# Softmax with a temperature on one core: a one-row tail on the sixth chunk's load and a one-row head on the first chunk's store

## The chip, the cores and the metric

The kernel runs on one core of a Trainium2 chip. The metric is the device time of one execution in microseconds (us); the lower the better. The median of three runs of the kernel before the change is 162.11 us (162.08 to 162.43).

## What is computed

The reference is a softmax over the last axis with temperature 0.5:

```python
x = randn(16, 1024, 512)  # float32
x_scaled = x / 0.5
x_max = max(x_scaled, axis=-1, keepdims=True)
exp_x = exp(x_scaled - x_max)
out = exp_x / sum(exp_x, axis=-1, keepdims=True)  # float32
```

There are 16,384 rows of 512 elements, 2 KB each. The input and the output are 33.55 MB each, and every byte is moved once.

## The kernel before

**Tiling.** The rows are cut into eight chunks (C = 8). A chunk has 128 partitions with G = 16 consecutive rows each, so that a whole chunk is 4 MB, 32 KB a partition, contiguous in memory for each partition. Six buffers (BUFS) hold chunks; the seventh and the eighth chunk take the buffers of the first and the second. Everything is done in place: a chunk is loaded, turned into its softmax, and stored from the same buffer.

**Lists.** Three lists say how a chunk is cut, by rows of a partition. LOADS gives the DMAs of its load, BLOCKS the pieces in which it is computed, STORES the DMAs of its store. Before the change, the first chunk is loaded in two parts (the first 4 rows of a partition, then the other 12), the next six whole, the eighth without its last two rows (LATE), which come on the Pool queue. The first chunk is computed in three blocks and the last in two, which makes eleven blocks in all. Every chunk is stored whole.

**Queues.** `load` (L65 holds its DMA) issues the loads of the first six chunks from ScalarE's queue, all at the start and in order, and those of the last two chunks from SyncE's queue, where each waits until the buffer's old chunk has been stored. `store` (L144) issues every store from ScalarE's queue. In that queue's ring, then, seven load DMAs of six chunks stand first, and all eight stores follow. `load_last_rows` (L87, L93) issues the eighth chunk's last two rows from the Pool queue.

**Work on a block.** `shift` takes the negated row maximum on VectorE (L74) and doubles it (L78). `exponentials` runs one ScalarE instruction a row, exp(2x - 2max) with the row's sum on the side (L104). `scale_vector` takes the reciprocal of the sums (L121) and multiplies most rows by it on VectorE (L123); `scale_scalar` scales the last eighth of the rows on ScalarE (L134). A store follows when the chunk's last block is done.

**Order.** The order of each engine's instructions is written by hand (manual_schedule). A loop over the blocks i issues the exponentials of block i + 1, the scaling of block i on both engines, the maximum of block i + 2, and the store of block i. For the second chunk the last two rows' exponentials are put behind the store of the first chunk, on ScalarE's queue.

**Semaphores.** DMAs from ScalarE's and SyncE's queues count their completion on eight semaphores that are taken in turn; a DMA that takes a semaphore again has to come after the earlier DMA on it has completed. At the end SyncE waits for everything.

Of the kernel before, what the change touches and what calls it, by code (L numbers as in the profile page):

```python
# [1 line left out]

# [4 lines left out]


@with_exitstack
def kernel(  # L10
    ctx: ExitStack,
    tc: tile.TileContext,
    x: bass.AP,
    out: bass.AP,
):
    nc = tc.nc
    fp32 = mybir.dt.float32
    P = nc.NUM_PARTITIONS
    AX = mybir.AxisListType.X
    EXP = mybir.ActivationFunctionType.Exp  # L20
    COPY = mybir.ActivationFunctionType.Copy
    MAX = mybir.AluOpType.max

    D = x.shape[-1]
    xf = x.flatten_outer_dims()
    of = out.flatten_outer_dims()
    N = xf.shape[0]

    G = 16
    C = N // (P * G)
    assert C * P * G == N
    xr = xf.rearrange("(c p g) d -> c p g d", p=P, g=G)
    outr = of.rearrange("(c p g) d -> c p g d", p=P, g=G)
    WHOLE = [(0, G)]
    LATE = 2
    LOADS = [[(0, 4), (4, G)]] + [WHOLE] * 6 + [[(0, G - LATE)]]
    BLOCKS = [[(0, 4), (4, 8), (8, G)]] + [WHOLE] * 6 + [[(0, 8), (8, G)]]  # L40
    STORES = [WHOLE] * 8
    BMAX = 16
    BUFS = 6

    data = ctx.enter_context(tc.tile_pool(name="data", bufs=BUFS))
    stats = ctx.enter_context(tc.tile_pool(name="stats", bufs=6))

    ctx.enter_context(tc.manual_schedule())


    chunks = {}
    blocks = [(c, lo, hi) for c in range(C) for lo, hi in BLOCKS[c]]
    n = len(blocks)
    biases, sums, recips = {}, {}, {}

    finished = []
    def load(c):
        if c < BUFS:
            chunks[c] = data.tile([P, G, D], fp32, name="xt")
        else:  # L60
            chunks[c] = chunks[c - BUFS]
        xt = chunks[c]
        queue = nc.scalar if c < BUFS else nc.sync
        for lo, hi in LOADS[c]:
            part = queue.dma_start(out=xt[:, lo:hi, :], in_=xr[c][:, lo:hi, :])  # L65
            finished.append(part.ins.name)

    def shift(i):
        c, lo, hi = blocks[i]
        if c not in chunks:  # L70
            load(c)
        b = hi - lo
        negmax = stats.tile([P, BMAX], fp32, name="negmax")
        nc.vector.tensor_reduce(  # L74
            negmax[:, 0:b], chunks[c][:, lo:hi, :], axis=AX, op=MAX, negate=True
        )
        biases[i] = stats.tile([P, BMAX], fp32, name="bias")
        nc.vector.tensor_scalar_mul(biases[i][:, 0:b], negmax[:, 0:b], 2.0)  # L78

    def load_last_rows(signal):
        seen = stats.tile([P, 1], fp32, name="seen", bufs=1)
        copied = nc.gpsimd.tensor_copy(out=seen, in_=signal)  # L87
        finished.append(copied.ins.name)
        c = C - 1
        to = chunks[c - BUFS][:, G - LATE : G, :]  # L90
        of_ = xr[c][:, G - LATE : G, :]
        for p0, p1 in ((P - 2, P), (0, P - 2)):
            part = nc.gpsimd.dma_start(  # L93
                out=to[p0:p1], in_=of_[p0:p1], max_dma_last_dim=4 * D
            )
            finished.append(part.ins.name)

    def exponentials(i, rows):
        c, lo, hi = blocks[i]
        if i not in sums:  # L100
            sums[i] = stats.tile([P, BMAX], fp32, name="sums")
        for g in rows:
            row = chunks[c][:, lo + g, :]
            nc.scalar.activation(  # L104
                out=row,
                in_=row,
                func=EXP,
                bias=biases[i][:, g : g + 1],
                scale=2.0,
                accum_out=sums[i][:, g : g + 1],  # L110
            )
            if c == BUFS - 1 and g == 10:
                load_last_rows(sums[i][:, g : g + 1])


    def scale_vector(i):
        c, lo, hi = blocks[i]
        b = hi - lo
        k = b - b // 8
        recips[i] = stats.tile([P, BMAX], fp32, name="recip")  # L120
        nc.vector.reciprocal(recips[i][:, 0:b], sums[i][:, 0:b])  # L121
        rows = chunks[c][:, lo : lo + k, :]
        last = nc.vector.tensor_mul(  # L123
            rows, rows, recips[i][:, 0:k].unsqueeze(2).broadcast_to((P, k, D))
        )
        if i == n - 1:
            finished.append(last.ins.name)

    def scale_scalar(i):
        c, lo, hi = blocks[i]  # L130
        b = hi - lo
        for g in range(b - b // 8, b):
            row = chunks[c][:, lo + g, :]
            last = nc.scalar.activation(  # L134
                out=row, in_=row, func=COPY, scale=recips[i][:, g : g + 1]
            )
            if i == n - 1:
                finished.append(last.ins.name)

    def store(i):  # L140
        c, _, end = blocks[i]
        for lo, hi in STORES[c]:
            if hi == end:
                part = nc.scalar.dma_start(  # L144
                    out=outr[c][:, lo:hi, :], in_=chunks[c][:, lo:hi, :]
                )
                if c < C - 1:
                    finished.append(part.ins.name)

    load(0)  # L150
    warm = stats.tile([P, 1], fp32, name="warm", bufs=1)
    nc.vector.memset(warm, 0.0)  # L152
    nc.scalar.activation(out=warm, in_=warm, func=EXP)  # L153
    for c in range(1, BUFS):
        load(c)

    shift(0)
    shift(1)

    def rows(i):  # L160
        c, lo, hi = blocks[i]
        cut = hi - lo - (2 if c == 1 else 0)
        return range(cut), range(cut, hi - lo)

    exponentials(0, rows(0)[0])
    for i in range(n):
        if i + 1 < n:
            exponentials(i + 1, rows(i + 1)[0])
        scale_vector(i)
        scale_scalar(i)  # L170
        if i + 2 < n:
            shift(i + 2)
        store(i)
        if i + 1 < n:
            exponentials(i + 1, rows(i + 1)[1])

    seen = nc.sync.nop()
    info = mybir.DependencyInfo(
        mybir.DependencyClass.Sync, mybir.DependencyReason.DATA
    )  # L180
    for name in finished:
        tc.add_manual_dep(seen.ins, name, info, reason="leaves one wait for the end")


# [1 line left out]
_INS = ['x']  # L186
_OUTS = [((16, 1024, 512), 'float32')]


# [23 lines left out]
```

## Time and profile before

| what | value |
| --- | --- |
| median of the runs | 162.11 us |
| profiled execution, its own time | 162.08 us |
| span from its first instruction to its last | 160.2 us |
| bytes moved | 67.13 MB, half read from memory, half written |
| mean DMA rate over the span | 419 GB/s |
| ScalarE queue's ring (q10) | 2160 packets, 58.72 MB |
| SyncE queue's ring (q1) | 288 packets, 7.86 MB |
| Pool queue's ring (q0) | 192 packets, 0.52 MB |

The profile shows one execution. DVE is VectorE, ACT is ScalarE, POOL is GpSimd, SP is SyncE. Each row of the sliced view divides the span into 40 equal slices of 4.0 us; a digit is the busy share in tenths, and the GB/s row gives what the 16 DMA engines moved in a slice. A window's row gives its start and end in us and its length, then for VectorE, ScalarE and GpSimd the busy time and the number of instructions, then the clock, the DMA busy share and the GB/s. A DMA packet is counted in the window in which it starts, so a share can be over 1. A transfer is made of packets, one a partition here, and ends on each DMA engine with a packet of 4 bytes that counts its completion. The chain of waits lists start, duration and instruction of the chain of work that ended last.

### The profile page before, as it was taken

What the parts mean: (1) busy time and instruction counts of PE and PEld (TensorE: products, weight loads), DVE (VectorE), ACT (ScalarE), POOL (GpSimd) and SP (SyncE); (2) the same over time, 40 slices, a digit from 0 to 9 for tenths busy, and PEclk for the clock granted to TensorE, in tenths of its full rate; (3) what the DMA queues carried; (4) which work ended last, traced back from release to release, by engine and by line L of the source; (5) the groups of instructions that cost most, each with busy time, mean ns of one, the idle gap of its engine ahead of it and who ended that gap; (6) DMA issues with size and microseconds to landing.
All of it is one profiled execution on the core that took longest, in us unless ns stands there. A gap on an engine that the chain in (4) does not pass through costs nothing.

```text
span 160.2 us, 410 instructions
## 1 busy us (share of the span) xinstructions
DVE 134.6 (84%) x45; ACT 102.2 (64%) x273; POOL 1.9 (1%) x7
## 2 busy tenths in 40 slices
DVE  0607999999999999999999999999999999958000
ACT  3071549069989972998199909991899891690000
POOL 0000000000000000000000000040000000000000
DMA  5999999999999997999999999999999999999995
GB/s 184 470 401 507 401 393 499 417 393 468 442 401 442 466 401 303 475 393 434 475 401 417 475 409 417 444 459 394 428 456 436 397 466 450 393 442 466 401 401 245
DMA packets 2642, 67.13 MB, mean 419 GB/s; under 512 B 336, under 2 KB 336, under 8 KB 464
## 3 DMA queue, kind: packets, MB, share of 16 engines
q10 hardware_dynamic: 2160, 58.72, 86.0%
q1 hardware_dynamic: 288, 7.86, 11.4%
q0 software_dynamic: 192, 0.52, 0.8%
q14 instruction: 2, 0.02, 0.0%
HBM read 33.55 MB, written 33.55 MB: 419 GB/s over the span
## 4 chain that ended last, share of the span: by engine, by line
DVE 76%; DMA 7%; issue 5%; ACT 3%; ACTq 0%
DVE negmax L74 42%; DVE xt L123 32%; DMA xt<-in_x_dram 7%; ACT xt L104 3%; DVE bias L78 1%; DVE recip L121 1%; ACTq L65 0%
## 5 line engine op out<-in xcount | busy, mean ns | idle before, releaser
L104 ACT ACTIVATE xt<-xt,bias 128x512 f32<-128x512 f32 x128 | 90.4, 708 | 40.7 <-DVE bias L78 39.8
L74 DVE TENSOR_REDUCE negmax<-xt 128x16 f32<-128x8192 f32 (+2 forms) x11 | 69.9, 6353 | 9.5 <-DMA xt<-in_x_dram 9.5
L123 DVE TENSOR_TENSOR xt<-xt,recip 128x7168 f32<-128x7168 f32 (+2 forms) x11 | 62.0, 5637 | 0.4
L104 ACT ACTIVATION_READ_ACCUMULATOR xt<-xt,bias 128x1 f32 x128 | 23.9, 187 | 0.0
L134 ACT ACTIVATE xt<-xt,recip 128x512 f32<-128x512 f32 x15 | 9.9, 706 | 0.0
L121 DVE RECIPROCAL recip<-sums 128x16 f32<-128x16 f32 (+2 forms) x11 | 2.4, 219 | 1.8 <-ACT xt L104 1.8
L153 ACT ACT_TABLE_LOAD x1 | 1.3, 1283 | 1.6 <-PEq L197 1.6
L78 DVE TENSOR_SCALAR bias<-negmax 128x16 f32<-128x16 f32 (+2 forms) x11 | 1.9, 173 | 0.4
L93 POOL DMA_DIRECT2D xt<-in_x_dram x2 | 1.5, 741 | 0.5 <-issue 0.5
L87 POOL COPY seen<-sums 128x1 f32<-128x1 f32 x1 | 0.2, 184 | 103.7 <-ACT xt L104 103.7
L152 DVE MEMSET warm<- 128x1 f32 x1 | 0.1, 59 | 0.8 <-PEq L197 0.8
L153 ACT ACTIVATE warm<-warm 128x1 f32<-128x1 f32 x1 | 0.2, 202 | 0.0
L197 POOL MEMSET const-bfloat16-1.0<- 128x1 bf16 x1 | 0.1, 96 | 0.0
L197 POOL MEMSET const-uint8-127<- 128x1 uint8 x1 | 0.1, 96 | 0.0
L197 POOL MEMSET const-float32-0.0<- 128x1 f32 x1 | 0.1, 93 | 0.2 <-issue 0.2
L197 POOL MEMSET const-float32-1.0<- 128x1 f32 x1 | 0.1, 93 | 0.0
## 6 DMA issues: line engine op xcount, KB each, us to landing
out_dram<-xt ACTq DMA_DIRECT2D x8, 4096.0 KB, 24.9
xt<-in_x_dram ACTq DMA_DIRECT2D x5, 4096.0 KB, 39.5
xt<-in_x_dram SPq DMA_DIRECT2D x1, 4096.0 KB, 23.6
xt<-in_x_dram SPq DMA_DIRECT2D x1, 3584.0 KB, 26.4
xt<-in_x_dram ACTq DMA_DIRECT2D x1, 3072.0 KB, 11.7
xt<-in_x_dram ACTq DMA_DIRECT2D x1, 1024.0 KB, 4.8
xt<-in_x_dram POOLq DMA_DIRECT2D x1, 504.0 KB, 20.9
xt<-in_x_dram POOLq DMA_DIRECT2D x1, 8.0 KB, 9.6
```

Source lines behind the costliest of these rows:

```text
L74: nc.vector.tensor_reduce(negmax[:, 0:b], chunks[c][:, lo:hi, :], axis=AX, op=MAX, negate=True)
L78: nc.vector.tensor_scalar_mul(biases[i][:, 0:b], negmax[:, 0:b], 2.0)
L87: copied = nc.gpsimd.tensor_copy(out=seen, in_=signal)
L93: part = nc.gpsimd.dma_start(out=to[p0:p1], in_=of_[p0:p1], max_dma_last_dim=4 * D)
L104: nc.scalar.activation(out=row, in_=row, func=EXP, bias=biases[i][:, g : g + 1], scale=2.0, accum_out=sums[i][:, g : g + 1],)
L121: nc.vector.reciprocal(recips[i][:, 0:b], sums[i][:, 0:b])
L123: last = nc.vector.tensor_mul(rows, rows, recips[i][:, 0:k].unsqueeze(2).broadcast_to((P, k, D)))
L134: last = nc.scalar.activation(out=row, in_=row, func=COPY, scale=recips[i][:, g : g + 1])
L152: nc.vector.memset(warm, 0.0)
L153: nc.scalar.activation(out=warm, in_=warm, func=EXP)
L197: nc = _bacc.Bacc("TRN2", target_bir_lowering=False, num_devices=1)
```

## The change

The sixth chunk's load is issued as two DMAs instead of one: the first 15 of each partition's 16 rows (30 KB), then the last row (2 KB). The first chunk's store is issued as two DMAs: each partition's first row alone (2 KB), then the other 15 (30 KB). Both parts of either go to the same queue as before, one right behind the other. The condition in `store` is changed so that all parts of a chunk's store are issued when its last block is done. Nothing else differs.

```diff
-    LOADS = [[(0, 4), (4, G)]] + [WHOLE] * 6 + [[(0, G - LATE)]]
+    LOADS = [[(0, 4), (4, G)]] + [WHOLE] * 4 + [[(0, G - 1), (G - 1, G)], WHOLE, [(0, G - LATE)]]
     BLOCKS = [[(0, 4), (4, 8), (8, G)]] + [WHOLE] * 6 + [[(0, 8), (8, G)]]
-    STORES = [WHOLE] * 8
+    STORES = [[(0, 1), (1, G)]] + [WHOLE] * 7
...
     def store(i):
         c, _, end = blocks[i]
         for lo, hi in STORES[c]:
-            if hi == end:
+            if end == G:
                 part = nc.scalar.dma_start(
                     out=outr[c][:, lo:hi, :], in_=chunks[c][:, lo:hi, :]
                 )
```

## The prediction, on record before the changed kernel ran

> **What bounds the kernel now.** I read the page first: busy shares, then the sliced DMA rows.
>
> ```profile
> DVE 134.6 (84%) x45; ACT 102.2 (64%) x273; POOL 1.9 (1%) x7
> ...
> DMA  5999999999999997999999999999999999999995
> GB/s 184 470 401 507 401 393 499 417 393 468 442 401 442 466 401 303 475 393 434 475 401 417 475 409 417 444 459 394 428 456 436 397 466 450 393 442 466 401 401 245
> ```
>
> The DMA engines have work in every slice, and one slice in the middle (the sixteenth, 60 to 64 us) drops to 303 GB/s. Single slices are uneven because a packet counts where it starts, and packets are big: a whole chunk goes as one 32 KB packet a partition, eight for each of 16 engines. So I cut the trace into windows of four rounds of such packets (4.84 us), and then around the dip into windows of one round (1.21 us). The last two columns are the DMA share and GB/s.
>
> ```profile
> 47.00:51.84 4.84, 4.84 (x1) 4.84 (x15) 0.00 (x0) 1.00 1.01 433
> 51.84:56.68 4.84, 4.84 (x2) 4.84 (x15) 0.00 (x0) 1.00 1.01 433
> 56.68:61.52 4.84, 4.84 (x1) 2.31 (x6) 0.00 (x0) 1.00 1.02 345
> 61.52:66.36 4.84, 4.77 (x4) 3.36 (x9) 0.00 (x0) 1.00 1.00 433
> ...
> 152.50:157.34 4.84, 0.00 (x0) 0.00 (x0) 0.00 (x0) 1.00 1.00 433
> ```
>
> ```profile
> 57.23:58.44 1.21, 1.21 (x1) 1.21 (x4) 0.00 (x0) 1.00 1.23 433
> 58.44:59.65 1.21, 1.21 (x1) 0.56 (x1) 0.00 (x0) 1.00 0.75 217
> 59.65:60.86 1.21, 1.21 (x1) 0.00 (x0) 0.00 (x0) 1.00 1.04 271
> 60.86:62.07 1.21, 1.21 (x1) 0.00 (x0) 0.00 (x0) 1.00 0.95 406
> 62.07:63.28 1.21, 1.14 (x4) 0.28 (x1) 0.00 (x0) 1.00 1.00 433
> ```
>
> Loads alone, loads beside stores, and stores alone all run at 433 GB/s: that is the pace of the kernel, and 67.13 MB at it are 154.9 us of the 160.2 us span. The one place in the middle where the pace breaks is 58.4 to 62.1 us. The three weak rounds lack (433 - 217) + (433 - 271) + (433 - 406) = 405 of 433, so 0.94 of a round or **1.13 us**. No engine is idle there (shares 0.75, 1.04, 0.95): packets in flight take longer. In the packet records the last load packet of each engine takes 1.88 to 2.43 us where the others take 1.21 to 1.22, and ten of the last but one take 1.39 to 1.81.
>
> What sits there? In the Activation queue's ring stand seven loads (two of the first chunk, one each of chunks 2 to 6) and behind them the stores. Counting completions (4-byte packets) puts the end of the sixth chunk's load at 61.33 to 62.48 us and the first chunk's store directly behind it. It is the only place where a ring goes from loads to stores: the later loads are on SyncE's ring and Pool's.
>
> Then the vector engine, which the chain of waits names:
>
> ```profile
> 113.02 7.63 DVE xt L123
> 120.64 4.34 DVE negmax L74
> ...
> 132.91 4.42 DVE negmax L74
> ...
> 143.58 3.89 DVE xt L123
> ```
>
> From 12.9 to 137.5 us VectorE has no gap worth the name (the "issue" of 6.36 us after 126.55 is the same multiplication seen twice: the timeline has it from 125.36 for 7.63). Its end frees the last store, issued at 147.56. The seventh store's completions fall between 147.58 and 149.33, so the last store comes hardly too early: **the end is set by the DMA engines, but VectorE stands less than 1 us behind.**
>
> **The change, part by part.**
>
> *The turn itself.* The ring's end of loads becomes 8 packets of 30 KB and 8 of 2 KB an engine, and its begin of stores 8 of 2 KB and 8 of 30 KB. I read the 1.13 us as reading ahead: while the last load packets are still being written, the engine already reads the first store packet, and the two share a path. Over the 16 engines 0.94 of a packet is lost on average, which suggests about one packet read ahead. If the read-ahead goes by packets, it shrinks to a 2 KB packet, 1/16: 1.13 x 1/16 = 0.07 us is left and 1.06 us goes. If it goes by bytes, the same 30 KB are read ahead through small packets and nothing goes. The trace can't tell them apart; bounds 0 and 1.06 us. I take the first, because the loss lies near one packet and differs between engines (0.66 to 1.38 us), which a buffer of fixed bytes would not explain.
>
> The Trainium skill (DMA: Bandwidth & Descriptors, "Two DMAs through the same engine are not ordered") says that an engine's read and write sides are separate queues and that descriptors of one queue are pipelined; that fits a read-ahead, but gives no price for a turn, and no run here shows the sides apart.
>
> *More packets.* Each engine gets 16 more data packets and 2 more completions. The nearest rows: a completion takes 9 ns; Pool's 4 KB packets take 159 ns, 151 of them at 433 GB/s, so some 8 ns of a packet's own. 16 x 8 + 2 x 9 = **0.15 us** added. Below, nothing excludes 0; above, packets of a ring that has just started: the window from 1.75 to 2.80 us moved 226 GB/s, a loss of (433 - 226) / 433 x 1.05 = 0.50 us. Bounds 0 and 0.50 us; I take 0.15, since the ring is not empty at the turn.
>
> The rule that speaks against the change is in the same page ("Anatomy of one DMA" and "Rules for kernel authors"): every DMA has a fixed part of about 2.0 us, so small transfers should be joined. Two more DMAs would then cost 4 us if it stood in the open, an estimate of 166 us. The row speaks otherwise: from 61.52 us on, right behind the completions of a whole load, the rate is 433 GB/s, so a queue with work behind a completion pays no fixed part.
>
> *Issues on the Activation queue.* The load's second part is issued behind the present seventh load, which starts at 3.84 us; five issues in a row take 0.42 to 0.70 us each. ScalarE's first exponential starts at 8.09, waiting for VectorE, which hides it. The first store is issued at 44.16 (0.35 us), ahead of the second chunk's last two rows, whose sums VectorE wants at 46.26. In the built program the one-row store waits for nothing but its place, behind the scaling of the chunk's last row (43.43 to 44.13), as the loads at 1.71 ran beside the table load; so I cost it at nothing. If that cover fails, the two rows end 0.35 later at 46.43, VectorE slips by about 0.2 us, and the last store is issued at 147.76. While the DMA engines set the end, that too is hidden; if they come forward, it counts in the cap below.
>
> *Waits.* Completions are counted on eight semaphores in turn; two more DMAs shift the turn. In the built program the third chunk's store now also waits for the fifth chunk's load, and the fourth's for the sixth's first part. Both landed by 62.5; the stores are issued at 75.64 and 92.26. VectorE's maximum over chunk 6 waits for two loads instead of one, at 87.40. The seventh chunk's load on SyncE (72.61) waits for both parts of the first store; it was released by the landing and moves with it, and the second store already stands in the ring (issued 59.03). All nothing. What is queued behind them loses only if a load came over 13 us later.
>
> *What is late next.* The last store can't start before its issue: 147.56 plus the lead from issue to first packet. The first load had 0.74 to 1.76, 1.02 us; the one engine that ran dry at 147.59 resumed at 148.40, 0.84 us. Eight rounds of 1.21 us follow: 158.08 to 158.26 for the last completion, now at 159.01. The gain is **capped at 0.75 to 0.93 us**.
>
> *The sum.* -1.06 + 0.15 = -0.91 us at the ring, which the cap cuts to between 0.75 and 0.91. The engine that lost least at the turn, 0.66 us, ends at 158.55 now and would end at 158.55 - 0.66 x 15/16 + 0.15 = 158.08, still inside the cap's window. I take 0.75. The profiled execution took 162.08 us (span 160.2, 1.9 around it); the median of the runs is 162.11, 0.03 apart. 162.1 - 0.75 = **161.35 us**. Measurement can tell about 0.2% (0.32 us) from no change.
>
> **The rivals.**
>
> *The turn costs the same (0.20).* Read-ahead by bytes, or a turn with a fixed price. For it: all 16 engines pay at once whatever their phase. Against it: the spread between engines. Then -0 + 0.15: 162.25, between 162.1 and 162.4.
>
> *The turn gets dearer (0.25): slower.* With 2 KB packets at the end of the loads and at the begin of the stores the engine has less in flight at the turn, and the store's first long packets start like those of a fresh ring. Place: 58 to 63 us, in the Activation ring. Price: the start row, 0.50 us, on top of an unchanged 1.13 and with the 0.15: 162.1 + 0.65 = 162.75; if both small parts start so, 163.25. It decides from the point at which the 16 small packets lose more than the large ones saved, 1.06 us in my reading, any loss over 0.3 where the turn stays. For it: the only short packets at a start (8 KB, from 1.76 us) ran at half pace for a microsecond. Against it: Pool's 4 KB packets ran between large ones without a break.
>
> *VectorE takes over (inside my forecast).* If the store's extra issue pushes VectorE by 0.2 us, the cap is 0.55 to 0.73: 161.4 to 161.55.
>
> **How the numbers follow.** Forecast 0.55, turn unchanged 0.20, dearer 0.25. The forecast's own range goes from the full cap, 162.1 - 0.93 = 161.15, to half of the turn left, 161.8. The whole range reaches over the unchanged turn into the dearer one up to its single start: 161.1 to 162.8; a little over 0.1 is left above. Faster by over 0.2% is the forecast without its tail, 0.54; within 0.2% takes the unchanged turn and that tail, 0.21; slower 0.25.
>
> **What would show it.** Rounds of 1.21 us between 57 and 64 us: right if they lack together under 0.3 of a round, wrong if 0.9 or more. Completions of the seventh store before 148.6 and a gap ahead of the last store's first packets show the cap. The last store's issue at 147.56 (to 147.8) shows VectorE unmoved. The prediction is wrong if the weak rounds stay, or if weak rounds appear around the 2 KB packets.

## The result, and the profile after

The changed kernel took 162.69 us (median of 8 runs, 162.46 to 162.85), the kernel before 162.18 us beside it (8 runs, 162.04 to 162.43). The ratio is 1.0028 with a 95% interval of 1.0019 to 1.0037: slower by about 0.3%, where 161.35 us was forecast. The profiled execution of the changed kernel took 162.73 us, with a span of 160.6 us; before it was 162.08 with 160.2. In this pair of executions 0.35 us of the difference lie inside the span and 0.3 us around it, where 1.9 us became 2.2. Over all runs (below) it is **some 0.1 us inside the span, hardly clear of scatter, and 0.3 us around it**.

These are the lines of the page after the change that answer to those before: the engines' busy time, the sliced DMA rows, and the packet counts.

```profile
DVE 134.6 (84%) x45; ACT 102.2 (64%) x273; POOL 1.9 (1%) x7
...
DMA  5999999999999999999999999998999999999994
GB/s 184 469 400 506 400 392 508 408 392 482 425 400 460 413 367 368 421 452 408 490 400 402 498 399 423 435 465 386 429 456 435 401 490 416 400 457 449 392 433 212
DMA packets 2930, 67.13 MB, mean 418 GB/s; under 512 B 368, under 2 KB 368, under 8 KB 752
```

VectorE's and ScalarE's busy times are the same to a tenth of a microsecond. There are 288 more packets: 256 of 2 KB and 32 completions of 4 bytes, the last line's growth from 464 to 752. The slice at 60 us that stood at 303 GB/s now stands at 368, but its neighbour fell to 367. The windows of one round show what became of the turn (columns as before: start and end, length, three engines, clock, DMA share, GB/s):

```profile
57.23:58.44 1.21, 1.21 (x1) 1.21 (x4) 0.00 (x0) 1.00 0.98 406
58.44:59.65 1.21, 1.21 (x1) 0.58 (x1) 0.00 (x0) 1.00 1.76 406
59.65:60.86 1.21, 1.21 (x1) 0.00 (x0) 0.00 (x0) 1.00 0.04 5
60.86:62.07 1.21, 1.21 (x1) 0.00 (x0) 0.00 (x0) 1.00 0.79 274
62.07:63.28 1.21, 1.14 (x4) 0.26 (x1) 0.00 (x0) 1.00 1.34 560
```

406 GB/s is the plain rate here, because a round's packet is 30 KB. The round from 59.65 is empty: hardly a packet starts, since all 16 engines are still busy with the last 30 KB load packet that they began in the round before (share 1.76). In the packet records it takes 1.69 to 2.65 us in place of 1.14. The 2 KB packets behind it then run mostly at 84 ns each. So the loss stands, and it stands in the long packets, ahead of the short ones. Against the plain 406 the rounds lack 401 + 132, less 154 made up behind: 0.93 of a round, more than the 0.9 that the prediction had named as the sign of being wrong.

The last store's issue came at 147.57 (147.56 before) and its first packets again run from 148.4, so VectorE did not move:

```profile
143.59 3.89 DVE L123 TENSOR_TENSOR xt<-xt,recip 128x3584 f32<-128x3584 f32 x1
147.57 0.34 ACTq L144 DMA_DIRECT2D out_dram<-xt  x1
```

The seventh store completed between 147.70 and 149.56 (147.58 to 149.33 before), the last one between 158.16 and 159.25 (158.15 to 159.01). The engines' mean came 0.21 us later. No gap opened ahead of the last store, because nothing had come forward.

### The profile page after: what moved, and what is told of

It is laid out like the page before. It is cut to its first block, busy times and chain, and to the rows that moved or that the text cites. A ratio compares the mean times of both kernels' runs of the same rounds, so it can differ in the third digit from the quotient of the medians.

```text
span 160.6 us, 412 instructions
## 1 busy us (share of the span) xinstructions
DVE 134.6 (84%) x45; ACT 102.2 (64%) x273; POOL 1.9 (1%) x7
## 4 chain that ended last, share of the span: by engine, by line
DVE 71%; issue 9%; DMA 7%; ACT 3%; ACTq 0%
DVE negmax L74 42%; DVE xt L123 27%; DMA xt<-in_x_dram 7%; ACT xt L104 3%; DVE bias L78 1%; DVE recip L121 1%; ACTq L65 0%
```

## The experiments

Three questions were asked: where the 1.1 us belong, what the packets cost, and what makes up the time around the span. The time around a span is a run's time less its span; means are over all runs of a kernel. Spans of single runs of one kernel scatter by 0.1 to 0.4 us (standard deviation), so two mean spans that differ by less than some 0.15 us are not clear of chance; the time around the span scatters by 0.01 to 0.07 us, but by 0.13 to 0.15 in the first three of the experiments below (2.02 to 2.44 from run to run). Packet records come from one profiled execution of each kernel. The kernel before had 160.37, 160.36, 160.43 and 160.37 as mean span in the four groups of runs beside which the others stood, and 1.88, 1.90, 1.88 and 1.90 around it.

| kernel | DMAs | median us | ratio to before, 95% | mean span | around |
| --- | --- | --- | --- | --- | --- |
| before | 19 | 162.2 | 1 | 160.4 | 1.89 |
| the change | 21 | 162.69 | 1.0028 (1.0019 to 1.0037) | 160.50 | 2.17 |
| the change, again | 21 | 162.66 | 1.0026 (1.0014 to 1.0038) | 160.55 | 2.18 |
| load split alone | 20 | 162.75 | 1.0033 (1.0021 to 1.0045) | 160.55 | 2.28 |
| store split alone | 20 | 162.55 | 1.0017 (1.0008 to 1.0026) | 160.33 | 2.26 |
| both splits elsewhere | 21 | 162.55 | 1.0021 (1.0010 to 1.0032) | 160.37 | 2.23 |
| loads on SyncE | 19 | 161.68 | 0.9964 (0.9952 to 0.9976) | 159.96 | 1.79 |
| 16 more instructions | 19 | 162.37 | 1.0006 (0.9997 to 1.0014) | 160.56 | 1.78 |
| two splits on SyncE's queue | 21 | 172.03 | 1.0605 (1.0591 to 1.0618) | 169.73 | 2.34 |
| change + loads on SyncE | 21 | 163.67 | 1.0072 (1.0052 to 1.0091) | 161.30 | 2.15 |
| early store | 20 | 162.32 | 1.0007 (0.9997 to 1.0016) | 160.35 | 2.02 |
| two unused DMAs, SyncE | 21 | 162.48 | 1.0012 (0.9997 to 1.0026) | 160.44 | 2.09 |
| two unused DMAs, ScalarE | 21 | 162.67 | 1.0023 (1.0012 to 1.0033) | 160.61 | 2.07 |
| store in five | 23 | 162.81 | 1.0036 (1.0023 to 1.0049) | 160.50 | 2.33 |
| change + 16 instructions | 21 | 163.30 | 1.0058 (1.0038 to 1.0078) | 161.03 | 2.16 |
| Pool's load whole | 18 | 163.50 | 1.0076 (1.0059 to 1.0093) | 161.45 | 2.11 |
| loads on SyncE, Pool's load whole | 18 | 162.28 | 1.0003 (0.9995 to 1.0012) | 160.53 | 1.78 |

### One half at a time, and both elsewhere

The first two kernels do one half of the change each, the third does both away from the turn. These three diffs are against the changed kernel.

```diff
-    STORES = [[(0, 1), (1, G)]] + [WHOLE] * 7
+    STORES = [WHOLE] * 8
```

> Only the sixth chunk's load is split; the first chunk's store is whole. Theory A (the turn reads ahead by bytes and costs the same 1.1 us, and each added DMA costs its own price wherever it stands): half of the 0.5 us of the change, about 162.4 us, three weak rounds near 60 us as before. Theory B (short packets at the turn make the turn itself dearer, above all in the store): the load part alone is nearly free, 162.2 us. Theory C (read-ahead by packets): would show a turn still dear here, since the first store packet is 32 KB, 162.3 us.

```diff
-    LOADS = [[(0, 4), (4, G)]] + [WHOLE] * 4 + [[(0, G - 1), (G - 1, G)], WHOLE, [(0, G - LATE)]]
+    LOADS = [[(0, 4), (4, G)]] + [WHOLE] * 6 + [[(0, G - LATE)]]
```

> Only the first chunk's store is split; the sixth chunk's load is whole. Theory A: about 162.4 us, the last 32 KB load packets of each engine as long as before (1.9 to 2.4 us). Theory B: nearly all of the change's price, 162.6 us. Theory C: the last load packets come back to about 1.3 us, as only 2 KB would be read ahead, and the time falls to about 161.5 us.

```diff
-    LOADS = [[(0, 4), (4, G)]] + [WHOLE] * 4 + [[(0, G - 1), (G - 1, G)], WHOLE, [(0, G - LATE)]]
+    LOADS = [[(0, 4), (4, G)]] + [WHOLE] * 2 + [[(0, G - 1), (G - 1, G)]] + [WHOLE] * 3 + [[(0, G - LATE)]]
...
-    STORES = [[(0, 1), (1, G)]] + [WHOLE] * 7
+    STORES = [WHOLE] * 4 + [[(0, 1), (1, G)]] + [WHOLE] * 3
```

> The same two splits, moved away from the turn: the fourth chunk's load (15 rows and 1) and the fifth chunk's store (1 row and 15). Theory A: the same price as the change, 162.6 to 162.7 us, with the turn as before at 58 to 62 us. Theory B: little, 162.2 to 162.3 us.

The load split alone took 162.75 us, as much as the whole change, where the three theories had 162.2 to 162.4. The store split alone took 162.55, near theory B's 162.6 and 0.15 over A's 162.4, and 1 us over C's 161.5. Both elsewhere took 162.55, between A's 162.6 and B's 162.3. The halves' prices, 0.53 and 0.33 us at the medians, do not add up to the change's 0.5.

The store split alone is the clean test of the step on which the forecast hung: the first store packet is 2 KB, the last load packet 32 KB. These are its rounds.

```profile
57.23:58.44 1.21, 1.21 (x1) 1.21 (x4) 0.00 (x0) 1.00 1.23 433
58.44:59.65 1.21, 1.21 (x1) 0.41 (x1) 0.00 (x0) 1.00 0.89 244
59.65:60.86 1.21, 1.21 (x1) 0.00 (x0) 0.00 (x0) 1.00 0.82 217
60.86:62.07 1.21, 1.21 (x1) 0.00 (x0) 0.00 (x0) 1.00 0.71 284
62.07:63.28 1.21, 1.14 (x4) 0.42 (x1) 0.00 (x0) 1.00 1.09 462
63.28:64.49 1.21, 1.21 (x1) 1.21 (x5) 0.00 (x0) 1.00 1.07 461
```

They lack (433 - 244) + (433 - 217) + (433 - 284), less 29 and 28 made up later: 497 of 433, 1.39 us by this count, in which the short packets' completions and uneven starts stand too. It is no less than before. By the packet records the way from the fifth chunk's last completion to the end of the first store took 20.48 us on the engines' mean, 20.47 before, and the last load packet of an engine still took 1.82 to 2.11 us. The mean span of this kernel's 11 runs is 160.33 us beside 160.37, where a turn at 1/16 of its loss would have brought it forward by up to the cap's 0.75. A read-ahead that goes by packets is out.

With both splits elsewhere the time went up as well, and its span not at all: 160.37 beside 160.37. Most of the price is not paid at the turn but around the span. What little there is inside went with the load split (160.55 against 160.37 in its group) and not with the store split (160.33). Where one ring works alone the packets' price can be read from the mean completions: the first store in two parts took 9.72 us in the changed kernel and 9.78 in the store split alone, 9.68 whole before, in five parts (below) 9.92. That is 0.04 to 0.10 us for one more DMA of 2 KB packets. A single 2 KB packet took 84 ns, where 433 GB/s would take 76.

### Another ring, and an earlier meeting

All loads go to SyncE's queue; then no ring goes from loads to stores:

```diff
-        queue = nc.scalar if c < BUFS else nc.sync
+        queue = nc.sync
```

> All loads are issued from SyncE's queue, so that no ring goes from loads to stores; nothing is split. If the loss of 1.1 us belongs to a turn inside one ring, the weak rounds near 60 us are gone; the ring then gains up to 1.1 us, and the issue of the last store at 147.56 caps the gain at 0.75 to 0.93 us: 161.3 us. If the loss belongs to any first meeting of loads and stores, it moves to where the first store starts, near 45 us, and the time stays at 162.2 us. If the interleaved loads come too late for VectorE, it is slower, over 163 us.

Its rounds near 60 us are full, and the weak ones stand where the first store starts (issued at 44.06):

```profile
44.92:46.13 1.21, 1.18 (x2) 1.08 (x4) 0.00 (x0) 1.00 1.45 433
46.13:47.34 1.21, 1.18 (x3) 1.07 (x3) 0.00 (x0) 1.00 0.37 108
47.34:48.55 1.21, 1.21 (x1) 1.21 (x5) 0.00 (x0) 1.00 1.24 433
48.55:49.76 1.21, 1.21 (x1) 1.21 (x4) 0.00 (x0) 1.00 0.96 406
49.76:50.97 1.21, 1.21 (x1) 1.21 (x5) 0.00 (x0) 1.00 0.94 406
...
59.65:60.86 1.21, 1.21 (x1) 0.00 (x0) 0.00 (x0) 1.00 1.00 433
```

(325 + 27 + 27) / 433 x 1.21 = 1.06 us, against 1.13 at the turn of before. So the loss does not need a turn within a ring: it went along with the first store. The kernel is nonetheless the fastest tried, 161.68 us, ratio 0.9964 (0.9952 to 0.9976): 0.4 us less inside the span and 0.1 around it. Its profile has the last completion 0.1 us earlier than before and its span was the longest of its five, so where the 0.4 us come from is not shown.

Next, an early store from SyncE's queue. `store` gets these lines ahead of its loop, and the first chunk's entry in STORES becomes [(4, G)]:

```diff
+        if i == 0:
+            part = nc.sync.dma_start(
+                out=outr[0][:, 0:4, :], in_=chunks[0][:, 0:4, :]
+            )
+            finished.append(part.ins.name)
```

> The kernel before, with the first chunk's first four rows stored from SyncE's queue as soon as they are ready (near 18 us, between the loads); the other twelve rows are stored as before. If the loss of 1.1 us is paid once, where stores first meet loads, weak rounds stand near 18 to 21 us and none at 58 to 62, and the span is as before, 160.3 us. If it is paid at each passage from loads alone to stores, it stands at both places, and the ring ends about 1 us later: span about 161.0 to 161.3, 163.1 us.

```profile
18.42:19.63 1.21, 1.21 (x1) 0.03 (x1) 0.00 (x0) 1.00 1.14 433
19.63:20.84 1.21, 1.21 (x1) 0.00 (x0) 0.00 (x0) 1.00 0.85 298
20.84:22.05 1.21, 1.21 (x1) 0.00 (x0) 0.00 (x0) 1.00 0.55 190
22.05:23.26 1.21, 1.14 (x4) 0.80 (x3) 0.00 (x0) 1.00 1.39 596
23.26:24.47 1.21, 1.21 (x1) 1.21 (x4) 0.00 (x0) 1.00 0.93 399
...
60.86:62.07 1.21, 1.21 (x1) 0.00 (x0) 0.00 (x0) 1.00 1.01 433
62.07:63.28 1.21, 1.14 (x4) 0.16 (x1) 0.00 (x0) 1.00 1.16 433
63.28:64.49 1.21, 1.21 (x1) 1.21 (x4) 0.00 (x0) 1.00 0.86 366
```

The weak rounds moved to 19.6 us, where they lack 135 + 243, less 163 made up and with 34 more behind: 249 of 433, 0.70 us. The passage near 63 us, the same from loads to stores in ScalarE's ring as before, lacks only 67 of 433, 0.19 us. The loss is paid mostly at the first store, and its place does not change the span: 160.35.

The change with its loads on SyncE was to show both findings together:

> The changed kernel with all loads from SyncE's queue: the two splits stay, but they no longer stand one behind the other in a ring, and ScalarE's program is shorter by the eight loads. Theory P: about as loads_sync, 161.7 us, with at most 0.15 us for the packets, 1.8 us around the span. Theory D: the change's 0.5 us on top of loads_sync, 162.2 us.

It missed: 163.67 us. The one-row store, issued at 39.59, stands alone in ScalarE's ring and meets the loads first; the long part follows. These are its rounds (the load packets are of 32 KB up to 51 us and of 30 KB, the sixth chunk's, behind):

```profile
43.71:44.92 1.21, 1.21 (x1) 0.79 (x3) 0.00 (x0) 1.00 0.76 323
44.92:46.13 1.21, 1.18 (x3) 0.90 (x5) 0.00 (x0) 1.00 0.74 317
...
49.76:50.97 1.21, 1.21 (x1) 1.21 (x4) 0.00 (x0) 1.00 1.07 460
50.97:52.18 1.21, 1.21 (x1) 1.21 (x5) 0.00 (x0) 1.00 1.44 460
52.18:53.39 1.21, 1.21 (x1) 1.21 (x5) 0.00 (x0) 1.00 1.34 364
53.39:54.60 1.21, 1.21 (x2) 1.21 (x5) 0.00 (x0) 1.00 0.38 152
```

The two low rounds at the top look like a first loss and are none. By the packet records the 2 KB store packets and the 32 KB load packets take turns from 43.3 us on, and none of the 107 load packets that start between 42.3 and 50.8 us takes over 1.24 us; a round counts a packet where it starts, and the small packets shift the starts. The loss comes later, ahead of the first long store packets (the earliest at 54.39): there the 30 KB load packets take up to 2.65 us in place of 1.14.

A count that does not hang on where a round is cut is the time by which the long load packets exceed their plain 1.21 us (1.14 for 30 KB), on the mean of the 16 engines. At the turn it is 1.09 us before, 1.05 with the change and 1.05 with the store split alone; with all loads on SyncE it is 1.00 near 47 us; with the early store, whose packets are 8 KB, 0.50 near 20 us and 0.21 near 62. Here it is 0.00 beside the 2 KB store packets and 1.06 where the long ones begin. So by these records what costs is not that loads and stores meet, but that long store packets begin. Two more such places in this kernel, near 84 and 104 us, cost 0.4 us each, where the kernel with its loads on SyncE alone has none. They make 0.8 of the 1.3 us by which its mean span is the longer; why they come was not settled.

### The time around the span

Several theories were tried in turn: the length of ScalarE's program (P), the number of DMAs (D, and H for those of two queues alone), the lie of the program (L), the splitting of a chunk (S), and the issuing queue.

```diff
     for c in range(1, BUFS):
         load(c)
+    for _ in range(16):
+        nc.scalar.activation(out=warm, in_=warm, func=COPY)
```

> The kernel before with 16 tiny ScalarE instructions on the warm-up tile behind the loads' issues, where ScalarE waits for the first chunk; no DMA is added. Theory P (the change costs little inside the span; most of its price lies outside the span and comes with the length of ScalarE's program, which is fetched in 8 KB pages): six such pages ahead of the first instruction instead of five, the time around the span 2.2 us instead of 1.88, the span as before at 160.3; 162.5 us. Theory D (each added DMA costs by itself): 1.88 us around the span, 162.2 us.

Around the span 1.78, less than before, though the trace has six 8 KB instruction packets ahead of the start instead of five, as the changed kernel has. The changed kernel's second profile has five of them and the same 2.18 around its span. The number of these packets, and with it theory P, is out. The span rose by 0.2, of which more below.

With the same 16 instructions the changed kernel did not come back either:

> The changed kernel with 16 tiny ScalarE instructions on the warm-up tile behind the loads' issues. Theory L (the time around the span hangs on the lie of the program in its pages, for which the 16 instructions alone gave 1.78): around the span 1.8 to 1.9, 162.4 us. Theory D: 2.05 to 2.2 around the span, 162.7 us.

2.16 around the span, 161.03 inside, 163.30 us in all: theory L is out too, and neither theory had the longer span.

Two more DMAs on SyncE's queue were to be a quiet addition (the seventh chunk in 15 rows and 1, the eighth in 7 and 7):

> The kernel before with two more DMAs on SyncE's queue instead of ScalarE's: the seventh chunk's load in 15 rows and 1, the eighth's in 7 and 7. Theory P: SyncE's program is short, so five pages ahead of the first instruction, 1.88 us around the span, span as before: 162.2 us. Theory D: 2.2 us around the span or a longer span, 162.5 to 162.7 us.

It tells nothing of the theories: the loads came late. This line of the waits shows VectorE starved (us in total, times, longest).

```profile
DVE negmax L74 <- DMA xt<-in_x_dram: 19.8, 4, 8.2
```

Of the 19.8 us that VectorE waited for loads, 9.5 stood before. In this kernel the eighth chunk went in 14 KB packets beside stores of 32 KB packets, and landed at 130.5 us instead of 114.0: by this one case the engines seem to share out packets, not bytes.

Two unused DMAs of 32 KB each, then, on either queue, behind the loads in the program's text:

```diff
+    spare = stats.tile([P, 2, D], fp32, name="spare", bufs=1)
+    for k in range(2):
+        part = nc.sync.dma_start(out=spare[0:16, k, :], in_=xf[16 * k : 16 * k + 16, :])
+        finished.append(part.ins.name)
```

> The kernel before with two more DMAs that the softmax doesn't use: 16 rows of 2 KB each into a spare tile, issued from SyncE's queue at the start. No chunk is split. Theory D (each added DMA costs time around the span, wherever it stands and however small it is): 2.1 to 2.2 us around the span instead of 1.88; the span within 0.15 of 160.35; 162.5 us. Theory S (the price around the span comes with splitting a chunk on ScalarE's queue): 1.8 to 1.9 around the span, 162.3 us.

2.09 around the span, and 160.44 inside, as before. Its turn is that of the kernel before, and yet its rounds there are nearly full:

```profile
58.44:59.65 1.21, 1.21 (x1) 0.94 (x2) 0.00 (x0) 1.00 1.08 433
59.65:60.86 1.21, 1.21 (x1) 0.00 (x0) 0.00 (x0) 1.00 1.14 406
60.86:62.07 1.21, 1.21 (x1) 0.00 (x0) 0.00 (x0) 1.00 1.03 433
```

By the count above the load packets lose 0.37 us at this turn; in the other kernels whose turn is as before (both splits elsewhere, 16 instructions, two splits on SyncE's queue, Pool's load whole) it is 0.92 to 1.30. So the 1.1 us are no fixed price, and what sets their size stays open. The span gained nothing by it. One reason in sight is the cap: the first chunk landed 0.35 us later beside the small loads (12.54 against 12.19 us), and the last store was issued at 147.94 in place of 147.56.

From ScalarE's queue (nc.scalar in place of nc.sync):

> The two unused 32 KB DMAs again, but issued from ScalarE's queue, behind the loads. Theory D: around the span as with the two from SyncE, 2.09, or as with the change, 2.17. If the issuing queue sets the price around the span (one more DMA on ScalarE's gave 2.26 to 2.28, on SyncE's 2.02 to 2.09): 2.2 or more. Span within 0.15 of 160.35, since the small loads stand in front of the turn: 162.5 to 162.6 us.

2.07. Nothing is split in either kernel, and in the first nothing stands at the turn, and 0.2 us come up around the span all the same; the issuing queue makes no difference there. In the second the two small loads stand in the ring right ahead of the first store, and its mean span of 160.61 missed the 0.15 that was expected. Four more DMAs, with the first store in four single rows and twelve:

> The first chunk's store in five DMAs (four of one row, one of twelve), its load whole: four more DMAs than before. Inside the span 32 more packets and 4 more completions an engine: 0.3 us by 8 and 9 ns each, 160.65. Theory D: around the span four times the step of one DMA, 0.14 us by the kernel with the early store: 2.45 us, 163.1 in all. Theory S: about 2.25 as with one split, 162.9.

2.33 around the span, between theory S's 2.25 and D's 2.45, and 160.50 inside, where 160.65 was expected. The changed kernel once more:

> The changed kernel once more, beside the others on one chip, for the time around its span. Theories D and S: 2.15 us around the span and a span 0.1 to 0.2 over that of before, 162.6 to 162.7 us. If the time around the span differs from chip to chip or from load to load, it lies elsewhere between 1.9 and 2.4.

2.18, after 2.17 in its first runs: for this program the part is steady from group to group. Of the change's price beside it, 160.55 - 160.43 = 0.12 us is inside, within the scatter of such means, and 2.18 - 1.88 = 0.30 us around.

Last, one DMA less: the loop over two ranges of partitions in `load_last_rows` becomes one over all.

```diff
-        for p0, p1 in ((P - 2, P), (0, P - 2)):
+        for p0, p1 in ((0, P),):
```

> The kernel before with the eighth chunk's last rows in one DMA on the Pool queue instead of two: one DMA less than before, the same bytes. Theory D (the time around the span grows and falls with the number of DMAs): 1.75 us around the span instead of 1.88; the span within 0.2 of 160.35; 162.1 us. Theory H (only DMAs issued from ScalarE's and SyncE's queues count there): 1.88.

> All loads from SyncE's queue and the eighth chunk's last rows in one DMA. Theory D: 1.65 us around the span and a span as with the loads on SyncE alone (159.96): 161.6 us. Theory H: 1.78 around the span, 161.7 us.

Around the span 2.11 and 1.78, and 163.50 and 162.28 us in all, where theory D had 1.75 and 1.65 around it and H 1.88 and 1.78: the number of DMAs is not the rule either. Every kernel that added a DMA has 2.02 or more, those with the number unchanged 1.78 to 1.90, but one with a DMA less has 2.11. **What sets the time around the span stays open**; that the change raised it by 0.3 us is measured.

## Why the prediction was wrong, point by point

- *What bounds the kernel*: right. 433 GB/s stands in every full round, and the kernels whose last completion came later in the profile had the longer span with it (160.18 us and a span of 161.4 with Pool's load whole).
- *The turn itself*: wrong, and this is the step that failed. It said the read-ahead goes by packets and shrinks to 1/16, -1.06 us. With 2 KB packets on the store's side alone, the way across the turn took 20.48 us where it took 20.47; with them on both sides the last long load packets took up to 2.65 us, and 1.05 us were lost in place of 1.09. The cause was misplaced as well: "a turn in one ring" does not describe it, since the loss went along with the first store to 46 us in another ring (1.06 us) and to 20 us with an early store, and, in the change with its loads on SyncE, did not come at all while the store's packets were 2 KB. It stands ahead of the first store packets of 8 KB and more, also where small ones lie between. That fits bytes read ahead, the reading that the prediction set aside, but what happens in the engines there was not shown, and the 0.37 us with two unused DMAs is left unexplained.
- The reason given for choosing the packets, that the loss differs between engines, did not bear it: it differs as much with the small packets (1.69 to 2.65 us). (The records have eleven of the last but one packets at 1.39 to 1.81 us, not ten; nothing hangs on it.)
- *More packets*: right. 0.15 us was said for two more DMAs, from 8 ns of a packet's own; the 2 KB packets took 84 ns against 76, the same 8 ns. The mean completions give 0.04 to 0.10 us for each DMA, and 0.12 is the span's rise. The single profiles differ by as much: 16 instructions without any DMA put 0.14 us on the way across the turn.
- *Issues and waits*: right in the price, nothing. The one-row store did not stand behind the scaling of the chunk's last row, as was said, but was issued at 39.95, beside other work; the second part came at 44.19 in place of 44.16, and VectorE ended within 0.02 us of before.
- *The cap*: not put to the test by the change, since the ring did not come forward, but its terms stand. In this profile as in that before, the engine that finishes the last store first does so 10.6 us after the store's issue (158.17 after 147.57, 158.15 after 147.56), where 10.5 to 10.7 was said; with two unused DMAs on SyncE, where the issue came at 147.94, it is 158.53.
- *The sum*: it took the 1.9 us around the span as a constant. That is the missing term, +0.3 us, the larger part of the price; its cause stays open.
- *The rivals*: "the turn costs the same" was the right one for the ring; its 162.25 lacked the term around the span, with which it would be 162.55. "The turn gets dearer" named a time near the measured one (162.75) by luck, not by its reason: the way across the turn took 20.68 us in the changed kernel, 0.21 more than before and not the 0.65 that it had, and of that 0.15 is the packets' own and the rest less than the 0.14 of the 16 added instructions.
- The prediction gives the Trainium skill's fixed part of about 2.0 us ("DMA: Bandwidth & Descriptors", "Anatomy of one DMA") for every DMA; that section has it for DMAs issued from GpSimd, and the two here are issued from ScalarE's queue. Carried over to them it is an estimate of 4 us. The runs show some 0.1 us inside the span and 0.3 around it.

## What to carry to other kernels

A dip in a rate names a moment, not a cause: before cutting what stands next to it, move it (another ring, an earlier start) and see whether it goes along. When an edit is worth less than 1 us, the time around the span belongs in the sum, as here it changed by 0.3 us with a few DMAs that no engine waited for. Look at the packets themselves before a low round is called a loss, since a round counts starts. And where 16 engines carry equal shares, look for the one that does more.

## What the runs showed of the hardware that had not been expected

**The slowest DMA engine sets the end, and it can be the one that also fetches instructions.** With Pool's last rows in one DMA instead of two, fifteen engines finish by 158.8 us, and one alone goes on for a packet:

```profile
157.00:158.81 1.81, 0.00 (x0) 0.00 (x0) 0.00 (x0) 1.00 0.59 253
158.81:160.20 1.39, 0.00 (x0) 0.00 (x0) 0.00 (x0) 1.00 0.05 24
```

The packets left in that second window are one of 32 KB and one completion, 160.18 us. In the profile before, the engine with the two 8 KB instruction packets (at 37.51 and 92.73 us, 0.31 us each, and up to 0.4 us for the packet behind) carried one of Pool's 4 KB packets where most others had nine, and ended with them at 158.9. (Packets are put down to engines by following each from end to start.) The two-part load of before costs a DMA and goes with 1.1 us less of span: 160.37 against 161.45. The 16 added instructions brought a third such packet, at 142.97 us, into the run, and their span rose by 0.2; whether by that packet is not shown, since in this profile its engine ended at 159.13 and another at 159.18. In the changed kernel with the 16 instructions the engine with the packet at 142.37 us did end alone, at 159.80, the others by 159.27.

**Loads and stores ran beside each other at no loss until long store packets began.** In the change with its loads on SyncE, 2 KB store packets took turns with 32 KB load packets from 43.3 to 50.8 us, and every load packet took 1.21 to 1.23 us. Ahead of the first long store packets load packets were stretched by 1.09 us an engine in ScalarE's ring and by 1.00 between two rings, with nothing split; but only by 0.37 in the kernel with two unused DMAs.
